# Gathering the small matmuls of a recurrence into longer runs in a two-layer decoder trunk

## The chip, the cores and the metric

The kernel runs on one core of a Trainium2 chip. The metric is the device time of one execution in microseconds (us). A core has a matrix engine (PE, with its weight loads shown as PEld), a vector engine (DVE), a scalar engine (ACT), a general engine (POOL) and DMA queues, of which most here are issued from SP. Each engine works through its own list of instructions in order and waits on semaphores for the others.

## The reference, cut to what matters

Two residual layers over 1024 tokens of width 1024, each with an RMSNorm that is shifted and scaled from a conditioning vector, followed by a final norm. Layer 0 has one input projection, from which eight heads of a delta-rule recurrence and a gated spatial mixer are fed; layer 1 is sliding-window attention. The change lies in the recurrence:

```
def step(S, inp):
    r_t, w_t, k_t, v_t, kk_t, a_t = inp
    sa = einsum('bhvk,bhk->bhv', S, -kk_t)
    S = S * w_t + sa * (kk_t * a_t) + v_t * k_t      # per head, 64 x 64
    y_t = einsum('bhvk,bhk->bhv', S, r_t)
    return S, y_t
```

The kernel computes it in blocks of 64 tokens: what happens inside a block becomes matrix products, and only the state goes from block to block.

## The kernel before, in words

**Units.** The recurrence is cut into 8 units: 4 pairs of heads (`j`) times 2 halves of the sequence (`half`), unit `un = 2*j + half`. A unit holds 8 blocks of 64 tokens and two heads, one head on partitions 0 to 63 and the other on 64 to 127 (`rows2`).

**Stages of a unit.** `front` (L493) prepares scaled inputs (tiles `AR`, `BK`, `SV`, `BR`, `PA`). `solve` (L595) makes the products `A`/`pM<-AR,BK`, then inverts a triangular matrix per block: DVE transposes into `LN` (L632), runs 15 steps of forward substitution (`pr`, `LT`, L645 and L646) and makes `ZT` (L650) and `Zq` (L653); PE then multiplies `pM<-ZT`, `pM<-Zq,M`, and after another DVE step, `Tq` (L681), `pM<-Tq`. In between it issues `p<-SV,AV` (L655 and on). `prep` (L709) makes the products `uw`, `mq` and `pn`. `scan` (L743) walks along the blocks: for each it multiplies the state with `AR[:, 0]` into the PSUM tile `chain`, and one DVE instruction (L758, a scalar_tensor_tensor into `PA`) makes the next state of it. This is called a hop. The output of a block, `py`, is the sum of two products, `AR[:, 1] x PA` (rows `py<-PA,AR`) and `BR x SV` (rows `py<-SV,BR`), one of each per head. `post` (L767) normalises `py`.

**Shapes.** The projections (`pproj` in layer 0, `op` in the output projections) are matmuls of 128x128 by 128x512 in fp32r; each leaves one row in the trace. The products of the recurrence are small plain fp32 matmuls: `chain`, `py<-PA,AR` and `p` have 64 rows and 64 columns, `py<-SV,BR` and `pn` 128 rows and 64 columns. Each fp32 matmul leaves two rows in the trace, so that "x4" in a row of the timeline is two matmuls.

**What sets the order.** In layer 0 the order of PE's list is made by a small planner in the kernel, `drive` (L1109). The stages are Python generators ("threads") with priorities: scan 0, prep and solve 1, fronts 2, the mixer's tails 4, the conditioning sums and output weights 5, the stream of input projections (`stream`, L912) 6, the output projection 7. A thread runs until it yields; `yield x` means that it is not called again before the planner's own clock has gone on by `x`; that clock goes forward by a cost per matmul (`cost`, L109). `yield 0.0` lets others in at once. When the small work has run up a debt over `LAT["debt"]`, the next ready projection goes ahead of it. So the projections fill what the stages leave: every projection matmul yields. Between two hops there is a `yield LAT["hop"]` of 1.3. The order of DVE's, ACT's and POOL's lists is made by the framework's scheduler from priorities, not by this planner.

**Lines that the change touches.** The yields at L661 (inside `p`), L668 (inside `pM<-ZT`), L718 (after each group of `uw`), L730 (after each group of `mq`), L739 (inside `pn`), and the loop of `scan`, L751 to L764.

Layer 1 and the output projections are not touched.

Of the kernel before, what the change touches and what calls it, by code (L numbers as in the profile page):

```python
# [11 lines left out]
F32 = mybir.dt.float32  # L12
# [3 lines left out]
ALU = mybir.AluOpType  # L16
# [4 lines left out]
P = 128  # L21
D = 1024
T = 1024
KC = 8
HT = 512
# [68 lines left out]
def tile_kernel(ctx, tc, x, cons, par, rows, ada, ada0, ew, wup, sgw, sgb, ewo, ow, owo, out, dbg=None):  # L94
# [14 lines left out]
    def cost(lhsT, rhs):  # L109
        n = math.prod(rhs.shape[1:])  # L110
        m = math.prod(lhsT.shape[1:])
        if rhs.dtype == F32R:
            return max(n if n >= 256 else 4 * n, m) / 2400.0
        return max(4 * n, 2 * m, 60) / 2400.0

    def mm(out, lhsT, rhs, **kw):
        clock[0] += cost(lhsT, rhs)
        last[0] = nc.tensor.matmul(out, lhsT=lhsT, rhs=rhs, **kw).ins  # L118
# [5 lines left out]
    V = nc.vector  # L124
# [8 lines left out]
    ps = pes.enter_context(tc.tile_pool(name="ps", bufs=2, space=PSUM, reuse_waits="tile"))  # L133
# [4 lines left out]
    def pm(name):  # L138
        return ps.tile([P, HT], F32, name=name, tag="m", bufs=2)
# [4 lines left out]
    def psc(name):  # L144
        return ps.tile([P, HT], F32, name=name, tag="sc", bufs=1)
# [128 lines left out]
            yield 0.0  # L274
        return pt

# [1 line left out]
    hp = ctx.enter_context(tc.tile_pool(name="hp", bufs=1, reuse_waits="tile"))  # L278

    def new_hh(half):  # L280
# [2 lines left out]
    def new_h():  # L283
        return [new_hh(half) for half in range(2)]

    h = new_h()
# [169 lines left out]
    y0d = dp.tile([P, KC, T], F32, name="y0d")  # L456
    gated = dp.tile([2, D], F32, name="gated")

# [1 line left out]
    gls = ExitStack()  # L460
    gl = gls.enter_context(tc.tile_pool(name="gl", bufs=1, reuse_waits="tile"))
    res = ExitStack()
# [5 lines left out]
    def RC(name, w):  # L468
        return rcon[:, CONSTS[name] - NC0:CONSTS[name] - NC0 + w]
# [3 lines left out]
    Sst = lp.tile([P, 64], F32, name="Sst")  # L473
    i2 = lp.tile([P, 64], F32, name="i2")
    G.tensor_tensor(out=i2, in0=ident[:, 0:64], in1=ident[:, 64:128], op=ALU.add)
    rows2 = (slice(0, 64), slice(64, 128))
# [118 lines left out]
    def solve(un):  # L595
        AR, BK = us[un]["AR"], us[un].pop("BK")
        yield LAT["sv0"]
        yield lambda: scannable[0] > un
        SV, BR, PA = (us[un][k] for k in ("SV", "BR", "PA"))
# [10 lines left out]
        for g in range(2):  # L610
            cg = slice(g * 4, g * 4 + 4)
            pts = [pm("A"), pM()]
            for i in range(4):
                c = g * 4 + i
                for hd in range(2):
                    hs = rows2[hd]
# [25 lines left out]
        for i in range(1, 16):  # L642
# [8 lines left out]
                        in1=RC("bm", 2).unsqueeze(2).unsqueeze(3).to_broadcast([P, 2, 8, 16]), op=ALU.mult)  # L651
# [5 lines left out]
        for c in range(8):  # L657
            for e in range(2):
                mm(pt[rows2[e], c * 64:c * 64 + 64], lhsT=AV[rows2[1 - e], c, :], rhs=SV[rows2[1 - e], c, e, :], start=True, stop=True, tile_position=(64 - e * 64, e * 64))
            if c == 3:  # L660
                yield 0.0  # L661
        S.activation(PA[:, :, 0, :], pt.rearrange("p (c v) -> p c v", c=8), AF.Copy)
        yield LAT["qt2"]
        p1 = pM()
        p2 = p1[:, 256:384].rearrange("p (c t) -> p c t", t=16)
        for c in range(8):
            if c == 4:
                yield 0.0  # L668
            for qd in range(4):
                a = qd * 32  # L670
                mm(p1[a:a + 32, c * 32:c * 32 + 32], lhsT=Df[a:a + 16, 112 + c * 16:144 + c * 16], rhs=ZT[a:a + 16, c, :], start=True, stop=True, tile_position=(a, a))
# [37 lines left out]
    def prep(un):  # L709
        u = us[un]  # L710
        AR, SV, BR, PA, dC = (u[k] for k in ("AR", "SV", "BR", "PA", "dC"))
        for g in range(2):
            cg = slice(g * 4, g * 4 + 4)
            pt = pm("uw")
            for i in range(4):
                mm(pt[:, i * P:(i + 1) * P], lhsT=Z[:, g * 4 + i, :], rhs=PA[:, g * 4 + i, :, :], start=True, stop=True)
            p4 = pt.rearrange("p (c a v) -> p c a v", c=4, a=2)
            yield 0.0  # L718
            S.activation(PA[:, cg, 1, :], p4[:, :, 1, :], AF.Copy)
            S.activation(SV[0:64, cg, 0, :], p4[0:64, :, 0, :], AF.Copy)  # L720
            S.activation(SV[64:128, cg, 1, :], p4[64:128, :, 0, :], AF.Copy)
        wdone[0] = un + 1
        yield LAT["uw"]
        for g in range(2):
            cg = slice(g * 4, g * 4 + 4)
            pt = pm("mq")
            for i in range(4):
                for e, hs in enumerate(rows2):
                    mm(pt[hs, i * P:(i + 1) * P], lhsT=PA[hs, g * 4 + i, 1, :], rhs=BR[hs, g * 4 + i, e, :, :], start=True, stop=True)
            yield 0.0  # L730
            p4 = pt.rearrange("p (c a v) -> p c a v", c=4, a=2)
            V.tensor_tensor(out=AR[:, 0, cg, :], in0=p4[:, :, 0, :], in1=i2.unsqueeze(1).to_broadcast([P, 4, 64]), op=ALU.add)
            V.tensor_tensor(out=AR[:, 1, cg, :], in0=p4[:, :, 1, :], in1=AR[:, 1, cg, :], op=ALU.add)
        pn = pm("pn")
        for c in range(8):
            for e, hs in enumerate(rows2):
                mm(pn[hs, c * 64:c * 64 + 64], lhsT=BR[:, c, e, 0, :], rhs=SV[:, c, e, :], start=True, stop=True)
            if c == 3:
                yield 0.0  # L739
        V.tensor_tensor(out=PA[:, :, 0, :], in0=pn.rearrange("p (c v) -> p c v", c=8), in1=dC.unsqueeze(2).to_broadcast([P, 8, 64]), op=ALU.mult)  # L740
        yield LAT["mq"]

    def scan(un):  # L743
        half, u = un % 2, us[un]
        AR, SV, BR, PA, dC = (u[k] for k in ("AR", "SV", "BR", "PA", "dC"))
        if half:
            V.tensor_copy(PA[:, 0, 1, :], Sst)
        else:
            V.tensor_copy(PA[:, 1, 1, :], PA[:, 0, 0, :])
        yield LAT["hop"]  # L750
        py = ps.tile([P, HT], F32, name="py", tag="y", bufs=1)  # L751
        pc = psc("chain")
        for c in range(8):
            yc = slice(c * 64, c * 64 + 64)
            if c >= 1 - half and c < 8 - half:
                for hs in rows2:
                    mm(pc[hs, yc], lhsT=AR[hs, 0, c, :], rhs=PA[hs, c, 1, :], start=True, stop=True)
                V.scalar_tensor_tensor(out=PA[:, c + 1, 1, :] if c < 7 else Sst, in0=pc[:, yc], scalar=dC[:, c:c + 1], in1=PA[:, c, 0, :], op0=ALU.mult, op1=ALU.add)  # L758
            for e, hs in enumerate(rows2):
                if c or half:  # L760
                    mm(py[hs, yc], lhsT=AR[hs, 1, c, :], rhs=PA[hs, c, 1, :], start=True, stop=False)
                mm(py[hs, yc], lhsT=BR[:, c, e, 1, :], rhs=SV[:, c, e, :], start=not (c or half), stop=True)
            if c < 7:
                yield LAT["hop"]  # L764
        return py

    def post(un, py):  # L767
# [198 lines left out]
    def solve_thread():  # L966
        for un in range(8):
            yield lambda: solvable[0] > un
            yield from prioritised(solve(un), BOOST)
            solved[0] = un + 1  # L970

    def scan_gen(un):
        py = yield from scan(un)
        scanned[0] = un + 1
        threads.append([1, post_gen(un, py), clock[0], None])
# [10 lines left out]
    def prep_thread():  # L986
        for un in range(8):
            yield lambda: solved[0] > un
            yield from prioritised(prep(un), BOOST)
            prepped[0] = un + 1  # L990
# [15 lines left out]
            yield from do_ada(layer, part)  # L1006
        done["ada"] = True

# [1 line left out]
    x1d = dp.tile([T, D], F32, name="x1d")  # L1010
    done = {}
    stored = [0]
# [133 lines left out]
    if "x1" in dbg:  # L1146
        nc.sync.dma_start(out=dbg["x1"], in_=x1d)

# [1 line left out]
    h = done["h1"]  # L1150
    ps = ctx.enter_context(tc.tile_pool(name="ps1", bufs=2, space=PSUM, reuse_waits="tile"))

# [4 lines left out]
    y = ypl.tile([P, KC, T], F32, name="y1")  # L1157
# [154 lines left out]
        for j in range(8):  # L1312
            nc.sync.dma_start(out=dbg["y1"][j], in_=y[:, j, :])

# [1 line left out]
    def half_tiles(name, tag, bufs, src, dt=F32):  # L1316
        ts = [at.tile([P, HT], dt, name=name, tag=tag, bufs=bufs) for n in range(2)]
        for n in range(2):
            nc.scalar.dma_start(out=ts[n], in_=src(slice(n * HT, (n + 1) * HT)))
        return ts  # L1320
# [95 lines left out]
```

## Time and profile before

| | |
|---|---|
| time of three runs | 1151.12, 1145.09 and 1151.21 us, median 1151.12 |
| profiled execution, first to last instruction | 1148.8 us; the page gives no time outside it |
| PE busy | 1083.1 us, 94% |
| DVE busy | 720.4 us, 63% |
| ACT busy | 526.8 us, 46% |
| POOL busy | 385.0 us, 34% |
| layer 0's stages | about 75 to 640 us of the span |
| the eight scans | the first chain matmul starts at 165.8 us, the last at 608.6 us |

The times are from one profiled execution. Busy is the time in which at least one instruction of the engine was under way; matmuls overlap, so that the cost of one is read from the distance between starts and not from its duration. In a row of the timeline stand the start, the duration, engine, line, operation, output and inputs, rows and columns, element count and number of rows merged, and in brackets the idle time ahead of it and what ended that. All matmuls of the helper `mm` stand under L118.

### The profile page before, as it was taken

To read this page: it belongs to the slowest core of one execution; us is meant where nothing else is said; L and a number is where in the kernel's file an instruction comes from. 1 tells how busy PE (TensorE), PEld (TensorE's weight loads), DVE (VectorE), ACT (ScalarE), POOL (GpSimd) and SP (SyncE) were. 2 spreads that over 40 slices of the span, in tenths; PEclk is the share of its full clock that TensorE was granted. 3 is DMA by queue.
4 is the path that set the end of the run, shared out by engine and by line. 5 is a ranking of instruction groups with operands and counts; after the bars stand their busy time and mean duration, and the time that the engine had idled before them with its cause. 6 is when DMAs were issued, how large, how long until landed. Compare 5 with 4: busy or idle time off the path is not lost.

```text
span 1148.8 us, 20773 instructions
## 1 busy us (share of the span) xinstructions
PE 1083.1 (94%) x7912; PEld 856.7 (75%) x7912; DVE 720.4 (63%) x1666; ACT 526.8 (46%) x1252; POOL 385.0 (34%) x474
## 2 busy tenths in 40 slices
PE   3799899999999998999999999999999999999997
PEld 2677677777776766677676778878888888878886
DVE  6966758575868584676735257774656654479754
ACT  5565435544454435354332122233656654477521
POOL 3652214131313222143234210024455554457301
PEclk7799999999999998999999999999999999999999
DMA  8710212112121211123333144331011001152131
GB/s 307 250 44 19 75 40 73 56 47 65 47 77 38 90 56 48 42 79 104 110 128 111 64 147 138 114 111 55 19 37 38 29 29 56 38 169 72 67 108 55
DMA packets 55131, 93.42 MB, mean 81 GB/s; under 512 B 5748, under 2 KB 15988, under 8 KB 55032
## 3 DMA queue, kind: packets, MB, share of 16 engines
q1 hardware_dynamic: 45032, 77.10, 20.6%
q10 hardware_dynamic: 10000, 15.01, 4.0%
q8 instruction: 62, 1.02, 0.4%
q14 instruction: 37, 0.30, 0.1%
HBM read 79.49 MB, written 12.59 MB: 80 GB/s over the span
## 4 chain that ended last, share of the span: by engine, by line
PE 80%; DVE 12%; ACT 4%; DMA 2%; issue 1%; POOL 1%; ACTq 0%; POOLq 0%; DVEq 0%; SPq 0%
PE pproj L118 38%; PE op L118 15%; PE py L118 5%; PE pM L118 2%; PE pS L118 2%; DVE acc L369 2%; PE po L118 2%; PE pT L1227 2%; PE uw L118 1%; PE mq L118 1%; PE chain L118 1%; PE p L118 1%; PE pn L118 1%; DVE adacc L848 1%; PE A L118 1%
## 5 line engine op out<-in xcount | busy, mean ns | idle before, releaser
L118 PE MATMUL pproj<-lo,whi 128*128 128x512 f32 x704 | 285.6, 406 | 0.0
L118 PE MATMUL pproj<-hi,whi 128*128 128x512 f32 x704 | 284.7, 404 | 0.7 <-ACT vt L1181 0.7
L118 PE MATMUL pproj<-hi,wlo 128*128 128x512 f32 x704 | 284.5, 404 | 0.3 <-POOL wlo L246 0.3
L246 POOL TENSOR_TENSOR wlo<-wraw,whi 128x512 fp32r<-128x512 f32 x86 | 115.7, 1366 | 209.3 <-ACT whi L245 206.2
L118 PEld LDWEIGHTS pproj<-hi,wlo 128*128 128x128 f32 x704 | 132.6, 188 | 28.5 <-issue 3.3
L118 PEld LDWEIGHTS pproj<-hi,whi 128*128 128x128 f32 x704 | 132.7, 189 | 27.0 <-ACT vt L1181 1.1
L118 PEld LDWEIGHTS pproj<-lo,whi 128*128 128x128 f32 x704 | 132.7, 188 | 26.4 <-issue 2.4
L245 ACT ACTIVATE whi<-wraw 128x512 fp32r<-128x512 f32 x102 | 58.9, 623 | 80.3 <-PE htp L122 31.6
L118 PE MATMUL op<-wo,whi 128*128 128x512 f32 x256 | 81.8, 400 | 1.7 <-ACT whi L245 1.7
L1217 ACT ACTIVATE Sx<-Sx,nm 128x257 f32<-128x257 f32 (+1 forms) x128 | 62.3, 489 | 27.2 <-DVE nm L1213 25.5
L1213 DVE CUSTOM_DVE_ANT_0 Sx<-pS,bias,nsink 128x256 f32<-128x256 f32 (+1 forms) x128 | 53.4, 463 | 30.7 <-PE pS L118 29.2
L1221 POOL TENSOR_SCALAR Sx<-Sx,rc 128x256 f32<-128x256 f32 (+1 forms) x128 | 60.0, 483 | 25.9 <-DVE rc L1219 21.4
L1233 DVE TENSOR_TENSOR PL<-pT,PH 128x512 fp32r<-128x512 f32 (+1 forms) x64 | 41.6, 654 | 30.2 <-ACT PH L1232 29.6
L848 DVE SCALAR_TENSOR_TENSOR adacc<-araw,cond,adacc 128x512 f32<-128x512 f32 x56 | 45.2, 808 | 22.5 <-DMA araw<-ada 22.4
L118 PEld LDWEIGHTS op<-wo,whi 128*128 128x128 f32 x256 | 48.8, 191 | 13.8 <-ACT whi L245 2.2
L118 PE MATMUL op<-hi,yh 128*128 128x512 f32 (+1 forms) x136 | 51.8, 381 | 0.4 <-ACT yh L1331 0.4
L118 PE MATMUL op<-hi,yl 128*128 128x512 f32 (+1 forms) x136 | 51.8, 381 | 0.4 <-DVE yl L1332 0.4
L118 PE MATMUL op<-wo,wlo 128*128 128x512 f32 x128 | 52.0, 406 | 0.0
L118 PE MATMUL op<-lo,yh 128*128 128x512 f32 (+1 forms) x136 | 51.6, 379 | 0.0
L213 POOL TENSOR_TENSOR st<-st,nhalf 128x1 f32<-128x1 f32 x16 | 10.4, 650 | 100.3 <-DVE st L212 100.3
L1232 ACT ACTIVATE PH<-pT 128x512 fp32r<-128x512 f32 (+1 forms) x64 | 35.7, 563 | 17.9 <-PE pT L1227 16.6
L1227 PE MATMUL pT<-con,Sx 128*128 128x128 f32 x240 | 41.2, 273 | 0.0
(310 smaller groups left out, 2257.9 us busy)
## 6 DMA issues: line engine op xcount, KB each, us to landing
araw<-ada SPq DMA_DIRECT2D x64, 256.0 KB, 2.8
wraw<-ew SPq DMA_DIRECT2D x50, 256.0 KB, 3.0
wraw<-ow SPq DMA_DIRECT2D x36, 256.0 KB, 2.9
adaraw<-ada SPq DMA_DIRECT2D x16, 512.0 KB, 5.9
x<-x SPq DMA_DIRECT2D x8, 512.0 KB, 5.6
woraw<-ewo SPq DMA_DIRECT2D x16, 256.0 KB, 3.2
xr<-x ACTq DMA_DIRECT2D x16, 256.0 KB, 3.5
wraw<-y0d SPq DMA_DIRECT2D x16, 256.0 KB, 3.3
```

The costliest lines, as they stand in the source:

```text
L118: last[0] = nc.tensor.matmul(out, lhsT=lhsT, rhs=rhs, **kw).ins
L213: G.tensor_tensor(out=st[:, 3:4], in0=st[:, 2:3], in1=nhalf[:, 0:1], op=ALU.pow)
L245: a = S.activation(hi[:, gs, :], raws[g], AF.Copy)
L246: b = E.tensor_tensor(out=lo[:, gs, :], in0=raws[g], in1=hi[:, gs, :].bitcast(F32), op=ALU.subtract)
L369: V.scalar_tensor_tensor(out=acc, in0=raw[:, i], scalar=c, in1=acc, op0=ALU.mult, op1=ALU.add)
L848: op = V.scalar_tensor_tensor(out=acc, in0=raw, scalar=cond[:, k:k + 1], in1=acc, op0=ALU.mult, op1=ALU.add)
L1213: V.tensor_tensor_reduce(out=Sx[:, e, off:2 * P], in0=pS3[:, e, 0:nk], in1=bias[e][:, off:], scale=1.0, scalar=nsink[:, hd:hd + 1], op0=AL ...
L1217: S.activation(pr[:, e, off:2 * P + 1], Sx[:, e, off:2 * P + 1], AF.Exp, bias=nm[:, e:e + 1], scale=-1.0, accum_out=sm[:, e:e + 1])
L1221: G.tensor_scalar(out=pr[:, e, off:2 * P], in0=pr[:, e, off:2 * P], scalar1=rc[:, e:e + 1], scalar2=0.5, op0=ALU.mult, op1=ALU.mult)
L1227: nc.tensor.transpose(pT4[:, kb, e, :], pr[:, e, kb * P:(kb + 1) * P], ident)
L1232: S.activation(PH[:, ks, :], pT2[:, ks, :], AF.Copy)
L1233: V.tensor_tensor(out=PL[:, ks, :], in0=pT2[:, ks, :], in1=PH[:, ks, :].bitcast(F32), op=ALU.subtract)
```

## The change

It takes five yields out, and writes the loop of `scan` in another order. A hop now holds the two chain matmuls and the DVE instruction alone. The 16 products `BR x SV` of a unit, which don't depend on the state, are issued in one batch in the hop of block 4, right behind its chain matmuls; the PSUM tile `py` is taken there. The 16 products `AR[:, 1] x PA` (14 in the first half of a sequence, where the first block has no state) come in one batch after the last hop and add onto the first batch. Only the first two matmuls of the first batch carry the start flag, and only the last two of the second batch the stop flag. The number of matmuls is the same, 6020 in PE's list.

```diff
         for c in range(8):
             for e in range(2):
                 mm(pt[rows2[e], c * 64:c * 64 + 64], lhsT=AV[rows2[1 - e], c, :], rhs=SV[rows2[1 - e], c, e, :], ...)
-            if c == 3:
-                yield 0.0
...
         for c in range(8):
-            if c == 4:
-                yield 0.0
             for qd in range(4):
...
-            yield 0.0
             S.activation(PA[:, cg, 1, :], p4[:, :, 1, :], AF.Copy)
...
-            yield 0.0
             p4 = pt.rearrange("p (c a v) -> p c a v", c=4, a=2)
...
                 mm(pn[hs, c * 64:c * 64 + 64], lhsT=BR[:, c, e, 0, :], rhs=SV[:, c, e, :], start=True, stop=True)
-            if c == 3:
-                yield 0.0
...
-        py = ps.tile([P, HT], F32, name="py", tag="y", bufs=1)
         pc = psc("chain")
-        for c in range(8):
+        for c in range(1 - half, 8 - half):
             yc = slice(c * 64, c * 64 + 64)
-            if c >= 1 - half and c < 8 - half:
-                for hs in rows2:
-                    mm(pc[hs, yc], lhsT=AR[hs, 0, c, :], rhs=PA[hs, c, 1, :], start=True, stop=True)
-                V.scalar_tensor_tensor(out=PA[:, c + 1, 1, :] if c < 7 else Sst, ...)
-            for e, hs in enumerate(rows2):
-                if c or half:
-                    mm(py[hs, yc], lhsT=AR[hs, 1, c, :], rhs=PA[hs, c, 1, :], start=True, stop=False)
-                mm(py[hs, yc], lhsT=BR[:, c, e, 1, :], rhs=SV[:, c, e, :], start=not (c or half), stop=True)
+            for hs in rows2:
+                mm(pc[hs, yc], lhsT=AR[hs, 0, c, :], rhs=PA[hs, c, 1, :], start=True, stop=True)
+            V.scalar_tensor_tensor(out=PA[:, c + 1, 1, :] if c < 7 else Sst, ...)
+            if c == 4:
+                py = ps.tile([P, HT], F32, name="py", tag="y", bufs=1)
+                for i in range(8):
+                    for e, hs in enumerate(rows2):
+                        mm(py[hs, i * 64:i * 64 + 64], lhsT=BR[:, i, e, 1, :], rhs=SV[:, i, e, :], start=i == 0, stop=False)
             if c < 7:
                 yield LAT["hop"]
+        for c in range(1 - half, 8):
+            for hs in rows2:
+                mm(py[hs, c * 64:c * 64 + 64], lhsT=AR[hs, 1, c, :], rhs=PA[hs, c, 1, :], start=False, stop=c == 7)
         return py
```

Two places show what it does to the lists. First PE's list in the scan of the last unit, before: one whole hop with the projections on either side.

```order
L118 MATMUL pproj<-hi,whi 128x512
L118 MATMUL chain<-PA,AR 64x64 x2
L118 MATMUL py<-PA,AR 64x64
L118 MATMUL py<-SV,BR 64x64
L118 MATMUL py<-PA,AR 64x64
L118 MATMUL py<-SV,BR 64x64
L118 MATMUL pproj<-lo,whi 128x512
```

The same scan in the changed kernel, the hops of blocks 4 and 5 (`adag` is a sum of the conditioning).

```order
L118 MATMUL chain<-PA,AR 64x64 x2
L118 MATMUL py<-SV,BR 64x64 x16
L118 MATMUL pproj<-hi,whi 128x512
L118 MATMUL pproj<-lo,whi 128x512
L118 MATMUL pproj<-hi,wlo 128x512
L118 MATMUL adag<-adacc,ones 1x512
L118 MATMUL chain<-PA,AR 64x64 x2
```

The four single `py` matmuls of a hop are gone from it, and one run of 16 stands in the hop of block 4.

Second DVE's list in the solve of the fifth unit, between the making of `Zq` and that of `Tq`, before (`mx` and `uT` belong to the mixer, `sqy` to `post`).

```order
L653 STREAM_TRANSPOSE Zq<-ZT 128x256
L835 SCALAR_TENSOR_TENSOR mx<-mix,prm,bst 128x512
L836 TENSOR_TENSOR uT<-mx,uT 128x512
L491 TENSOR_TENSOR sqy<-py,niy 128x512
L679 TENSOR_TENSOR Zq<-Zq,pM 128x8x16
L687 COPY Z<-Zq 32x8x32 x2
L681 STREAM_TRANSPOSE Tq<-Zq 128x256
```

The same stretch in the changed kernel, from `Zq` on (`krv` is an evacuated projection, `adacc` a conditioning sum, `bv` and `gz` belong to `post` and `front`).

```order
L653 STREAM_TRANSPOSE Zq<-ZT 128x256
L303 SCALAR_TENSOR_TENSOR krv<-pproj,prm,krv 128x511
L842 SCALAR_TENSOR_TENSOR adacc<-araw,cond,adacc 128x512
L829 SCALAR_TENSOR_TENSOR mx<-mix,prm,bst 128x512
L830 TENSOR_TENSOR uT<-mx,uT 128x512
L775 SCALAR_TENSOR_TENSOR bv<-yc,der,bv 128x512
L976 SCALAR_TENSOR_TENSOR gz<-bv,der,gz 128x512
L592 TENSOR_TENSOR bv<-bon,krv 128x512
```

Between `Zq` and the addition to it (`Zq<-Zq,pM`) three instructions stood before, and in the changed kernel ten do: the seven shown, then another `adacc` and the two instructions of another `krv`.

More of the change, by code (lines that the diff above doesn't have):

```diff
@@ L750, in scan @@
         yield LAT["hop"]
-        py = ps.tile([P, HT], F32, name="py", tag="y", bufs=1)
         pc = psc("chain")
-        for c in range(8):
+        for c in range(1 - half, 8 - half):
             yc = slice(c * 64, c * 64 + 64)
-            if c >= 1 - half and c < 8 - half:
-                for hs in rows2:
-                    mm(pc[hs, yc], lhsT=AR[hs, 0, c, :], rhs=PA[hs, c, 1, :], start=True, stop=True)
-                V.scalar_tensor_tensor(out=PA[:, c + 1, 1, :] if c < 7 else Sst, in0=pc[:, yc], scalar=dC[:, c:c + 1], in1=PA[:, c, 0, :], op0=ALU.mult, op1=ALU.add)
-            for e, hs in enumerate(rows2):
-                if c or half:
-                    mm(py[hs, yc], lhsT=AR[hs, 1, c, :], rhs=PA[hs, c, 1, :], start=True, stop=False)
-                mm(py[hs, yc], lhsT=BR[:, c, e, 1, :], rhs=SV[:, c, e, :], start=not (c or half), stop=True)
+            for hs in rows2:
+                mm(pc[hs, yc], lhsT=AR[hs, 0, c, :], rhs=PA[hs, c, 1, :], start=True, stop=True)
+            V.scalar_tensor_tensor(out=PA[:, c + 1, 1, :] if c < 7 else Sst, in0=pc[:, yc], scalar=dC[:, c:c + 1], in1=PA[:, c, 0, :], op0=ALU.mult, op1=ALU.add)
+            if c == 4:
[3 more added lines that the diff above has]
+                        mm(py[hs, i * 64:i * 64 + 64], lhsT=BR[:, i, e, 1, :], rhs=SV[:, i, e, :], start=i == 0, stop=False)
             if c < 7:
                 yield LAT["hop"]
+        for c in range(1 - half, 8):
+            for hs in rows2:
+                mm(py[hs, c * 64:c * 64 + 64], lhsT=AR[hs, 1, c, :], rhs=PA[hs, c, 1, :], start=False, stop=c == 7)
         return py
```

## Prediction

> **What bounds the kernel now.** I read the page first, for the span, the busy shares and the engines of the chain that ended last.
>
> ```profile
> span 1148.8 us, 20773 instructions
> PE 1083.1 (94%) x7912; PEld 856.7 (75%) x7912; DVE 720.4 (63%) x1666; ACT 526.8 (46%) x1252; POOL 385.0 (34%) x474
> PE 80%; DVE 12%; ACT 4%; DMA 2%; issue 1%; POOL 1%; ACTq 0%; POOLq 0%; DVEq 0%; SPq 0%
> ```
>
> PE is the bound: it works for 94% of the span and carries 80% of the chain. That is an average over stages, so I read the table by windows for layer 0, where the change lies. Its columns are the stretch, its length, then busy time of PE, PEld, DVE, ACT and POOL, and the granted PE clock.
>
> ```profile
> 200.00:320.00 120.00, 116.08 (x1185) 86.25 (x1184) 80.42 (x188) 55.64 (x129) 30.85 (x23) 1.00 0.17 54
> 440.00:560.00 120.00, 113.76 (x1048) 82.94 (x1047) 75.14 (x173) 50.43 (x117) 34.52 (x25) 0.96 0.23 73
> ```
>
> PE is busy for 114 to 116 of 120 us there, DVE for 75 to 80. So a microsecond of PE's work that goes in this stage comes off the end, unless PE then waits for DVE.
>
> Busy does not mean well used. The timeline of PE shows one hop of a scan with the projections around it.
>
> ```profile
> 545.52 0.39 PE L118 MATMUL pproj<-hi,wlo 128*128 128x512 f32 x1
> 545.75 0.39 PE L118 MATMUL pproj<-hi,whi 128*128 128x512 f32 x1
> 546.07 0.33 PE L118 MATMUL chain<-PA,AR 64*64 64x64 f32 x4
> 546.24 0.28 PE L118 MATMUL py<-PA,AR 64*64 64x64 f32 x2
> 546.44 0.33 PE L118 MATMUL py<-SV,BR 128*64 128x64 f32 x2
> 546.70 0.32 PE L118 MATMUL py<-PA,AR 64*64 64x64 f32 x2
> 546.96 0.33 PE L118 MATMUL py<-SV,BR 128*64 128x64 f32 x2
> 547.21 0.50 PE L118 MATMUL pproj<-lo,whi 128*128 128x512 f32 x1
> 547.55 0.40 PE L118 MATMUL pproj<-hi,wlo 128*128 128x512 f32 x1
> ```
>
> A projection starts 0.23 us after the one before. From 545.75 to 547.55 two such steps would take 0.46; it takes 1.80, so the hop costs 1.34. The four single `py` matmuls, 546.24 to 547.21, take 0.97 of it: 0.20 to 0.26 each, whenever the row count changes between 64 and 128. The same shapes in unbroken runs are far cheaper. Eight `pn` matmuls between projections, and 16 `p` matmuls:
>
> ```profile
> 583.39 0.51 PE L118 MATMUL pproj<-hi,whi 128*128 128x512 f32 x1
> 583.83 0.69 PE L118 MATMUL pn<-SV,BR 128*64 128x64 f32 x16
> 584.45 0.50 PE L118 MATMUL pproj<-lo,whi 128*128 128x512 f32 x1
> 584.78 0.39 PE L118 MATMUL pproj<-hi,wlo 128*128 128x512 f32 x1
> 541.37 1.15 PE L118 MATMUL p<-SV,AV 64*64 64x64 f32 x32
> 542.45 0.50 PE L118 MATMUL pproj<-lo,whi 128*128 128x512 f32 x1
> ```
>
> Eight take 0.62 to the next start and 16 take 1.08, so one more of its kind costs 0.46 / 8 = 0.058 us. The groups by form, for the whole kernel, give the number of matmuls (two rows each) and their busy time:
>
> ```profile
> L118 PE MATMUL py<-SV,BR 128*64 128x64 f32 x256 | 40.8, 246 | 0.0
> L118 PE MATMUL py<-PA,AR 64*64 64x64 f32 x240 | 36.3, 231 | 0.0
> L118 PE MATMUL pn<-SV,BR 128*64 128x64 f32 x256 | 11.0, 228 | 0.0
> ```
>
> `pn` multiplies as many matrices of the same shape as `py<-SV,BR` and is busy for 11.0 us against 40.8.
>
> **The change part by part.** The price of a hop that holds its two chain matmuls alone has no row. The nearest is two matmuls of one form between projections:
>
> ```profile
> 163.38 0.39 PE L118 MATMUL pproj<-hi,wlo 128*128 128x512 f32 x1
> 163.70 0.34 PE L118 MATMUL py<-SV,BR 128*64 128x64 f32 x4
> 163.97 0.50 PE L118 MATMUL pproj<-hi,whi 128*128 128x512 f32 x1
> 164.31 0.39 PE L118 MATMUL pproj<-lo,whi 128*128 128x512 f32 x1
> ```
>
> 0.93 less two steps of 0.23 is 0.47. Of it 0.35 belong to coming from and going back to projections (0.47 less 2 x 0.058).
>
> *Removed from the scans:* 56 hops fall from 1.34 to 0.47, 48.7 us. In the four second halves block 7 has only `py`: 1.34 less the chain's 0.17 (546.07 to 546.24), 4.7 us. In the four first halves block 0 is the visit just priced, 1.9. Together 55.3.
>
> *Added:* 248 matmuls in batches at 0.058, 14.4; eight changes of form from the chain to the first batch at 0.26, 2.1; four last batches stand alone between projections (in the first halves they follow the chain matmuls, of the same form), 4 x 0.35 = 1.4. Together 17.9. Bounds for one batched matmul: 0.058 as in `p` and `pn`, 0.26 as in `py` now. I take 0.058, since `pn` is the same instruction as `py<-SV,BR` but for the flags, and projections that add onto a tile follow each other at their steady 0.23. Net of the scans 37.4.
>
> *The five other runs.* In the order `pn` was split in all 8 units and is whole in all; `p` was split in 4, `pM<-ZT` in 3, `mq` in 2, `uw` in 1. Two visits of eight cost 0.93 each (583.39 to 584.78 less two steps), one of 16 costs 0.93 + 0.46. A merge saves 0.47, and 18 of them 8.5. Only `pn` and `p` show this; for the other three forms I take the same.
>
> *Runs that now stand together.* The whole order has 380 stretches of projections before and 335 after. 22 of the 45 are accounted for (18 merges, 4 block-0 visits). The other 23, such as `pn` now straight behind `mq`, save between 0.35 - 0.26 = 0.09 and 0.35: 2 to 8 us, I take 3, nearer the low end because the neighbours differ in form.
>
> Sum: 37.4 + 8.5 + 3 = 49 us less work on PE, which makes 1148.8 - 49 = 1100.
>
> *What is late next.* DVE. Its work is not less. I read the table by windows for the seven stretches from a unit's `LN` to its `pM<-ZT`, units 2 to 8; two of the seven and the sum:
>
> ```profile
> 343.60:376.90 33.30, 32.53 (x252) 23.68 (x249) 28.50 (x69) 13.68 (x27) 14.47 (x10) 1.00 0.15 51
> 536.60:562.40 25.80, 25.80 (x200) 18.91 (x199) 21.63 (x59) 5.92 (x11) 9.01 (x6) 1.00 0.35 110
> sum 214.00, PE 208.66 PEld 150.83 DVE 176.00 ACT 81.61 POOL 77.74; mean PE 29.81 PEld 21.55 DVE 25.14 ACT 11.66 POOL 11.11
> ```
>
> DVE is busy in 176 of 214 us. A scan lies in each stretch, so PE's 208.7 fall by about 37.4 / 8 + 0.24 = 4.9 each, 35 in all, to 174. Were DVE's list the same, PE would stand there. In the changed order DVE's lists between `LN` and `ZT` hold 370 instructions in these units instead of 411; at 28.50 / 69 = 0.41 each, 17 us move out, and DVE needs 159 of 174. The slack falls from 33 to 15 us, and not evenly: units 3, 5 and 7 keep 59, 61 and 58 instructions, and between `Zq` and `Tq` the fifth now has ten others where it had three. What slack of 33 let through, the groups of waits tell, and who waits in the hops:
>
> ```profile
> PE pM L118 <- DVE Tq L681: 8.1, 4, 2.8
> DVE PA L758 <- PE chain L118: 32.2, 31, 2.9
> ```
>
> New waits at `ZT` and `Tq`: at best 8 us go with the present ones, at worst all 35 are given back; I take 12, a third. Behind a `pM` that waits stands all of PE's list, the projections too.
>
> *The hops themselves.* The chain matmuls of one hop, DVE's answer, and an instruction of DVE of the wide kind:
>
> ```profile
> 165.78 0.33 PE L118 MATMUL chain<-PA,AR 64*64 64x64 f32 x4
> 166.16 0.28 DVE L758 SCALAR_TENSOR_TENSOR PA<-chain,dC,PA 128x64 f32<-128x64 f32 x1
> 563.10 0.72 DVE L848 SCALAR_TENSOR_TENSOR adacc<-araw,cond,adacc 128x512 f32<-128x512 f32 x1
> ```
>
> The distance between hops falls from 2.95 (1.34 and seven steps of 0.23) to 2.1. In 31 of 56 hops DVE was waiting for the chain, so there is no queue ahead of it. In the other 25 a DVE instruction of about 0.72 us may stand ahead; 0 to 18 us, I take 3, since the state is there 0.66 us after the hop's start (166.16 + 0.28 - 165.78) and 1.4 of the 2.1 are spare.
>
> *The clock.* One wait of the present four was followed by a lower granted clock:
>
> ```profile
> 443.17 0.63 PE L118 MATMUL pM<-Tq,N 32*32 32x32 f32 x6 [2.71 <-DVE Tq L681]
> 440.00:454.00 14.00, 11.20 (x102) 9.35 (x101) 4.47 (x7) 6.30 (x16) 2.42 (x2) 0.63 0.23 76
> 570.35 0.69 PE L118 MATMUL pM<-Tq,N 32*32 32x32 f32 x32 [2.75 <-DVE Tq L681]
> 560.00:640.00 80.00, 74.51 (x640) 56.45 (x639) 38.41 (x65) 25.85 (x53) 31.72 (x23) 1.00 0.41 129
> ```
>
> (1 - 0.63) x 14 = 5.2 us were lost after the first wait of 2.7 us, while the clock stayed at 1.00 from 560 to 640, around the wait of 2.75 us. With more waits I expect one more such loss or none: -5 to +10, I take 3. [...]
>
> Forecast: 1100 + 12 + 3 + 3 = 1118 us. The median of the three runs lies 2.3 above the profiled span, less than my terms are known to; I leave it out. A measurement of this kernel can tell about 0.5%, 6 us, from no change.
>
> **Rivals.** *DVE takes all of the stretches.* The 35 us come back as waits at `ZT` and `Tq`: 1148.8 - 14 = 1135. For it: slack of 15 us in seven stretches with one in-order queue. Against: 41 instructions have left them.
>
> *No new wait.* The two `Tq` waits and the clock loss go as well, since both were chance meetings: 1100 - 8 - 5 = 1087, or 1095 if half of that. Against: three units keep their DVE load.
>
> *Slower, by the clock.* Each unit has two places where PE can wait on DVE, 16 in all. If PE, run short, stopped there for 2.7 us with the loss of 5.2 us each time, a stop costs 7.9 us, and beyond six stops the 49 us are gone; at eight it is 1100 + 63 = 1163. For it: slack halves. Against: one of the two long waits cost no clock, and no projection is scarce. [...]
>
> *It does not do what it says.* Matmuls that add onto an open `py` tile run no faster in a batch, at 0.2: 248 x 0.2 = 50, so the scans gain 55.3 - 50 - 2.1 - 1.4 = 2, the other runs 11.5, and waits of the size above take 12: 1147. Against: nothing in `pn`'s rows.
>
> **How the numbers follow.** Forecast with its neighbourhood 0.71, DVE takes all 0.14, no new wait 0.06, slower by the clock 0.05, no effect 0.04. Faster by over 0.5%: 0.71 + 0.14 + 0.06 = 0.91; within: 0.04; slower: 0.05. The range goes from 1098, the sum with hardly a wait, to 1136, all stretches given back; outside lie the two last cases, most of the no-wait case and little more.
>
> **What would show it.** `py` busy falls from 77 us to under 25 in the groups by form, a hop's visit reads about 0.47, `pn` stands as one x32 row, and layer 1 lasts as long as now. PE's waits for `ZT` and `Tq` grow from 8 us to about 20, DVE's wait for the chain shrinks. I am wrong if `py` in a batch steps at over 0.1 us, if hops wait for DVE by more than 10 us, or if waits elsewhere, such as for ACT, take the gain.

## The result, and the profile after

The changed kernel takes 1120.39 us (median of 4 runs, 1118.01 to 1120.78) against 1151.16 us for the kernel before (median of 4, 1145.09 to 1151.59). The ratio is 0.9746, with a 95% interval of 0.9718 to 0.9773: 2.5% faster, 31 us. The forecast was 1118 us.

The page of the changed kernel, the lines that answer to the three shown first of before:

```profile
span 1119.0 us, 20771 instructions
PE 1038.8 (93%) x7912; PEld 833.5 (74%) x7912; DVE 716.3 (64%) x1666; ACT 526.6 (47%) x1252; POOL 382.5 (34%) x474
PE 44%; DVE 1%; DMA 1%; ACT 0%; issue 0%; POOLq 0%; DVEq 0%; SPq 0%; ACTq 0%
```

PE's busy time fell by 44.3 us and the span by only 29.8, so PE now stands idle for longer. (The profiled run took 1120.78 us, 1.8 more than its span.) The chain was followed through less than half of the span here, so its shares can't be set beside those of before.

The change lies in layer 0, so the account is made there, from 75 us to the first matmul of the output projection. The windows of before and then of the changed kernel, one stretch each (length, then busy time of PE, PEld, DVE, ACT and POOL, then the granted clock):

```profile
75.00:661.80 586.80, 560.09 (x5226) 419.11 (x5225) 367.65 (x810) 249.60 (x561) 172.13 (x125) 0.99 0.22 68
```

```profile
75.00:634.30 559.30, 517.15 (x5230) 396.16 (x5229) 363.98 (x810) 250.26 (x561) 169.23 (x125) 0.98 0.23 71
```

From such a row three numbers follow. *Waits* are length less PE busy: 26.7 before, 42.2 after. *Clock* is half of the time for which the trace grants half the clock, taken from the single records, since the column has two digits: 5.1 before, 10.9 after. *Work* is PE busy less the clock's share: 555.0 before, 506.3 after. So the work fell by 48.7 us, waits took 15.4 back and the clock 5.8. What follows layer 0 went from 487.0 to 484.7 us (1148.8 - 661.8 and 1119.0 - 634.3). All the later tables use these three.

The split has limits. It counts half clock also while PE waits: counted only while PE is busy, 0.1 to 3.2 us pass from clock to work, depending on the kernel, so that differences in work of under 3 us are not told apart. And each split describes the one run that was profiled: the four runs of the changed kernel had a mean granted clock of 0.976 to 0.991, and the profiled one is that with 0.976.

*The matmuls.* The groups by form, after:

```profile
L118 PE MATMUL pn<-SV,BR 128*64 128x64 f32 x256 | 9.2, 224 | 1.2 <-DVE AR L727 0.8
L118 PE MATMUL py<-SV,BR 128*64 128x64 f32 x256 | 9.2, 225 | 0.0
L118 PE MATMUL py<-PA,AR 64*64 64x64 f32 x240 | 8.7, 220 | 0.3 <-DVE PA L748 0.3
```

The two `py` groups are busy for 17.9 us instead of 77.1, and `py<-SV,BR` now costs what `pn` costs. The timeline of PE, a first batch of 16, one hop, and a last hop with its batch of 14:

```profile
166.69 1.15 PE L118 MATMUL py<-SV,BR 128*64 128x64 f32 x32
167.77 0.50 PE L118 MATMUL pproj<-lo,whi 128*128 128x512 f32 x1
...
280.87 0.39 PE L118 MATMUL pproj<-lo,whi 128*128 128x512 f32 x1
281.19 0.33 PE L118 MATMUL chain<-PA,AR 64*64 64x64 f32 x4
281.45 0.50 PE L118 MATMUL pproj<-hi,wlo 128*128 128x512 f32 x1
281.78 0.39 PE L118 MATMUL pproj<-hi,whi 128*128 128x512 f32 x1
...
283.26 0.33 PE L118 MATMUL chain<-PA,AR 64*64 64x64 f32 x4
283.42 0.98 PE L118 MATMUL py<-PA,AR 64*64 64x64 f32 x28
284.34 0.50 PE L118 MATMUL pproj<-hi,whi 128*128 128x512 f32 x1
```

A hop costs 281.78 - 280.87 less two steps of 0.23, 0.45 us, where it cost 1.34. The 16 matmuls of a first batch take 1.08 to the next start, as `p` did. The 14 of a last batch, which add onto what the first batch wrote, take 0.92.

*The waits.* What PE waited for in layer 0 (total, times, longest), first two groups of before that the prediction did not show, then the changed kernel:

```profile
PE bkt L122 <- DVE BK L541: 3.0, 1, 3.0
PE pM L118 <- ACT N L628: 2.1, 6, 0.8
```

```profile
PE pM L118 <- DVE nsk L488: 5.4, 2, 3.1
PE pM L118 <- ACT N L628: 4.2, 6, 2.6
PE bkt L122 <- DVE BK L541: 4.1, 3, 2.7
PE pM L118 <- DVE Tq L677: 2.6, 3, 1.1
...
PE pproj L118 <- POOL wlo L246: 2.4, 2, 2.1
...
PE chain L118 <- DVE PA L748: 1.1, 3, 0.5
```

No group grew by much. There are 29 stops of over 0.5 us where there were 20, on DVE, ACT and POOL alike. The stop of 3.1 us put down to `nsk` is a `Tq` stop: the timeline of DVE ahead of it, and the matmul that waited.

```profile
303.33 0.28 DVE L675 TENSOR_TENSOR Zq<-Zq,pM 128x128 f32<-128x128 f32 x1
303.53 0.68 DVE L487 TENSOR_REDUCE nsk<-sqk 128x8 f32<-128x512 f32 x1
304.12 0.74 DVE L976 SCALAR_TENSOR_TENSOR gz<-bv,der,gz 128x512 f32<-128x512 f32 x1
304.90 0.59 DVE L683 COPY Z<-Zq 32x256 f32<-32x256 f32 x2
305.50 0.45 DVE L677 STREAM_TRANSPOSE Tq<-Zq 128x256 f32<-128x256 f32 x1
305.87 0.13 DVE L488 TENSOR_SCALAR nsk<-nsk 128x8 f32<-128x8 f32 x1
306.09 0.74 PE L118 MATMUL pM<-Tq,N 32*32 32x32 f32 x20 [3.13 <-DVE nsk L488]
```

The matmul reads `Tq`; `nsk` is only the DVE instruction that ended last ahead of it. Two strangers, `nsk` and `gz`, stood ahead of `Tq` and cost 1.4 us. The other `nsk` stop, 2.26 us at 431.8, is at a `pM<-Tq` too. The `nsk` and `Tq` groups together make 8.0 us, against 8.1 at `Tq` before.

*The solve stretches.* The same seven stretches as in the prediction, from `LN` to `pM<-ZT`, two and the sum:

```profile
339.00:372.70 33.70, 25.93 (x226) 18.74 (x228) 30.69 (x68) 17.53 (x35) 16.86 (x12) 0.95 0.24 77
517.40:542.10 24.70, 24.70 (x213) 18.02 (x216) 19.20 (x55) 6.58 (x12) 9.18 (x7) 0.95 0.33 106
...
sum 189.00, PE 173.03 PEld 127.34 DVE 161.31 ACT 81.25 POOL 72.51; mean PE 24.72 PEld 18.19 DVE 23.04 ACT 11.61 POOL 10.36
```

PE's 173.0 and DVE's 161.3 are what the prediction worked out (174 and 159). The first of the two is a stretch in which DVE is now the busier engine: PE is busy for 25.9 of 33.7 us, where before it was 32.5 of 33.3, and DVE for 30.7. The other is still full of PE's work.

*The clock.* The two longest spells at half clock, as windows around them:

```profile
300.00:318.00 18.00, 14.75 (x167) 11.94 (x156) 8.15 (x17) 7.34 (x19) 2.37 (x3) 0.72 0.14 46
509.00:521.00 12.00, 9.37 (x65) 6.60 (x63) 8.26 (x19) 5.58 (x16) 3.77 (x3) 0.72 0.35 111
```

(1 - 0.72) x 18 = 5.0 us went behind the wait of 3.13 us, and 3.4 us behind one of 2.63.

### The profile page after: what moved, and what is told of

It reads as the page before. It is cut to its first block, busy times and chain, and to the rows that moved or that the text cites. A ratio compares the mean times of both kernels' runs of the same rounds, so it can differ in the third digit from the quotient of the medians.

```text
span 1119.0 us, 20771 instructions
## 1 busy us (share of the span) xinstructions
PE 1038.8 (93%) x7912; PEld 833.5 (74%) x7912; DVE 716.3 (64%) x1666; ACT 526.6 (47%) x1252; POOL 382.5 (34%) x474
## 5 line engine op out<-in xcount | busy, mean ns | idle before, releaser
L118 PEld LDWEIGHTS pproj<-hi,wlo 128*128 128x128 f32 x704 | 133.4, 189 | 28.3 <-POOL wlo L246 3.3
L1211 ACT ACTIVATE Sx<-Sx,nm 128x257 f32<-128x257 f32 (+1 forms) x128 | 62.3, 489 | 27.7 <-DVE nm L1207 25.8
L842 DVE SCALAR_TENSOR_TENSOR adacc<-araw,cond,adacc 128x512 f32<-128x512 f32 x56 | 48.7, 869 | 27.5 <-DMA araw<-ada 27.3
L645 DVE TENSOR_TENSOR pr<-Lf,LT 128x2 f32<-128x2 f32 (+14 forms) x120 | 45.2, 376 | 2.6
```

The costliest lines, as they stand in the source:

```text
L645: V.tensor_tensor(out=pr[:, 0:nc_, 0:i + 1], in0=Lf[:, i:i + 1, 0:i + 1].to_broadcast([P, nc_, i + 1]), in1=LTt[:, 0:nc_, 0:i + 1], op=ALU ...
L842: op = V.scalar_tensor_tensor(out=acc, in0=raw, scalar=cond[:, k:k + 1], in1=acc, op0=ALU.mult, op1=ALU.add)
L1211: S.activation(pr[:, e, off:2 * P + 1], Sx[:, e, off:2 * P + 1], AF.Exp, bias=nm[:, e:e + 1], scale=-1.0, accum_out=sm[:, e:e + 1])
```

## The experiments

The theory: PE's work falls by its price per visit and per change of form, and what is given back is waits, above all for DVE, with the clock behind them. Its rivals are named with each pair. The table has every run, with layer 0 taken apart as above (each from one profiled run; the medians are of 4 to 10). What follows layer 0 took between 481.9 and 488.8 us in these profiles, though no run edits it, so a few us between two profiles mean little.

| kernel | median us | ratio to before | layer 0 | waits | clock | work |
|---|---|---|---|---|---|---|
| before | 1151.16 | | 586.8 | 26.7 | 5.1 | 555.0 |
| changed | 1120.39 | 0.9746 [0.9718, 0.9773] | 559.3 | 42.2 | 10.9 | 506.3 |
| yields alone | 1148.24 | 0.9989 [0.9966, 1.0013] | 592.1 | 32.0 | 13.7 | 546.5 |
| scan alone | 1134.86 | 0.9868 [0.9830, 0.9905] | 571.7 | 45.6 | 13.7 | 512.4 |
| sorted in the hop | 1126.53 | 0.9796 [0.9764, 0.9829] | 567.4 | 31.1 | 10.2 | 526.0 |
| crossed in the hop | 1151.04 | 1.0015 [0.9992, 1.0037] | 588.8 | 27.7 | 5.1 | 556.0 |
| changed, light DVE | 1109.90 | 0.9640 [0.9622, 0.9658] | 547.8 | 36.3 | 4.4 | 507.1 |
| before, light DVE | 1149.33 | 0.9978 [0.9958, 0.9999] | 589.1 | 24.7 | 11.3 | 553.1 |
| batch behind `pn` | 1130.86 | 0.9831 [0.9813, 0.9849] | 571.1 | 53.4 | 14.5 | 503.2 |
| longer pauses | 1121.14 | 0.9737 [0.9713, 0.9760] | 551.1 | 33.4 | 13.9 | 503.8 |
| pause before `kt` | 1137.51 | 0.9890 [0.9857, 0.9922] | 583.5 | 50.2 | 33.4 | 499.9 |
| `kt` and `qt1` | 1118.04 | 0.9707 [0.9681, 0.9733] | 555.5 | 39.8 | 11.9 | 503.8 |
| changed, again | 1122.19 | 0.9756 [0.9721, 0.9790] | 557.7 | 41.0 | 11.9 | 504.8 |

### The two halves of the change

The first kernel is the changed one with the scan of before, so that only the five yields are gone; the second is the kernel before with the new scan alone.

```diff
 # yields alone: after, with the loop of scan as before
-        for c in range(1 - half, 8 - half):
+        for c in range(8):
...
 # scan alone: before, with the loop of scan as after; the five yields stay
-        for c in range(8):
+        for c in range(1 - half, 8 - half):
...
```

> Only the five yields are taken out; the scan stays as before. Theory (going between projections and small matmuls costs PE about 0.35 us a visit): 34 stretches of projections fewer in the order, 18 of them merges at 0.47 us and 16 at 0.09 to 0.35, so 10 to 14 us less work on PE, and 2 to 4 us of new waits: span about 1140, ratio 0.990 to 0.995. Rival (only the forms inside a hop cost, visits are free): within 2 us of before.

> Only the scan's loop is written anew; the five yields stay. Theory: 37 us less work on PE and about 11 us of new waits, span about 1123, ratio 0.975 to 0.980; py busy for 18 us instead of 77. Rival (the two parts need each other, since the projections between the split runs were the cover for DVE): this alone gives clearly less wait and nearly all of the gain, under 1120.

The yields alone make no difference that can be told, 0.9989 [0.9966, 1.0013]; the theory's time was missed. Their work did fall by 8.5 us, and `pn` by form reads as in the changed kernel (9.2 us). In the profiled run waits took 5.3 and the clock 8.5; that run, 1151.25 us, lies 3 above the median of its ten. The windows of this kernel, layer 0 and its three longest spells at half clock:

```profile
75.00:667.10 592.10, 560.14 (x5246) 425.77 (x5244) 365.39 (x814) 252.41 (x563) 172.29 (x127) 0.98 0.22 69
440.00:454.00 14.00, 10.87 (x93) 8.71 (x93) 6.35 (x14) 4.32 (x11) 1.64 (x1) 0.63 0.25 77
530.00:541.00 11.00, 8.22 (x45) 6.22 (x46) 7.43 (x19) 5.18 (x16) 5.06 (x4) 0.69 0.46 143
620.00:630.00 10.00, 9.42 (x39) 6.30 (x38) 5.15 (x5) 4.52 (x9) 6.11 (x6) 0.66 0.32 97
```

PE's busy time is that of before to 0.1 us (560.14 and 560.09), because half clock stretches the matmuls by what the merges took off them: work fell by 8.5 us, and the clock's share rose from 5.1 to 13.7. (In the changed kernel a projection steps at 0.23 us where the trace grants the full clock, and at 0.42 to 0.43 from 307.68 to 309.38, in a spell at half clock.) Only the clock's column tells the two apart.

The scan alone gives 42.5 us less work, 5 more than forecast, and 1134.86 us, about 10 above what the theory gave for it (a span of 1123, to which 1.8 come): in the profiled run, the shortest of its four, waits rose by 18.9 us and the clock's loss by 8.5. So the theory holds for the work of both halves, nearly (8.5 + 42.5 = 51.0 against 48.7 together), and fails for the time of both: they save 3 and 16 us where both together save 31. What is given back is no fixed share of the gain.

### Why a `py` matmul was dear: change of form, or the add

The first kernel keeps all of a hop's matmuls in the hop and only sorts them by form. The second keeps the four changes of form, but lets no matmul follow the one that it adds onto: each pair is crossed with the other head's.

```diff
 # sorted: before, with
             for e, hs in enumerate(rows2):
-                if c or half:
-                    mm(py[hs, yc], lhsT=AR[hs, 1, c, :], ...)
+            if c or half:
+                for hs in rows2:
+                    mm(py[hs, yc], lhsT=AR[hs, 1, c, :], ...)
+            for e, hs in enumerate(rows2):
                 mm(py[hs, yc], lhsT=BR[:, c, e, 1, :], ...)
...
 # crossed: before, in the order AR x PA of head 0, BR x SV of head 1,
 # AR x PA of head 1, BR x SV of head 0
```

> Kernel before with the four py matmuls of a hop sorted: the two of 64 rows, then the two of 128. No batch, the same number of visits; 120 changes of form fewer. Theory (a change of form costs 0.2 us): 24 us less work on PE, 5 to 8 us of new waits, span 1130 to 1133, ratio about 0.985. Rival (it is the visit between projections, or the length of a run, that costs): no change, 1148.

> Kernel before with the four py matmuls of a hop crossed: the form still changes at each, but no matmul adds onto the words that the one ahead of it wrote. Theory (the change of form costs): no change, 1146 to 1152. Rival (a matmul that adds onto what the last one wrote has to wait for it): as much as 24 us less, 1130.

Sorting saves 29.0 us of work, 5 more than its theory gave, and about 24 us of time (0.9796 [0.9764, 0.9829]); crossing saves nothing (1.0015 [0.9992, 1.0037]), and its `py` groups read 40.8 and 36.3 us as before. The timeline of the sorted kernel, one hop:

```profile
530.41 0.39 PE L118 MATMUL pproj<-lo,whi 128*128 128x512 f32 x1
530.73 0.33 PE L118 MATMUL chain<-PA,AR 64*64 64x64 f32 x4
530.89 0.28 PE L118 MATMUL py<-PA,AR 64*64 64x64 f32 x4
531.11 0.34 PE L118 MATMUL py<-SV,BR 128*64 128x64 f32 x4
531.37 0.50 PE L118 MATMUL pproj<-hi,wlo 128*128 128x512 f32 x1
531.71 0.40 PE L118 MATMUL pproj<-hi,whi 128*128 128x512 f32 x1
```

The hop is 531.71 - 530.41 less two steps of 0.23, 0.84 us instead of 1.34: two changes between 64 and 128 rows are gone from each of 60 visits, 29.0 / 120 = 0.24 us each. So the price is the change of the row count, not the add onto an open tile. What PE does in these 0.24 us no run shows.

This small edit is worth more than it looks. With 13.6 us less work saved than by the new scan alone it is 8 us faster (1126.53 and 1134.86), and it has most of the time that the whole change saves.

### Do the waits come from DVE's load

Both kernels leave out seven of the eight pieces of the conditioning sums that run through layer 0 (the loads stay), so DVE has 44 us less to do in the changed kernel's layer 0 and 39 less in that of before.

```diff
-                if k:
-                    op = V.scalar_tensor_tensor(out=acc, in0=raw, scalar=cond[:, k:k + 1], in1=acc, ...)
-                else:
-                    op = V.tensor_scalar(out=acc, in0=raw, scalar1=cond[:, 0:1], ...)
-                paced(op)
+                if k == KC - 1:
+                    paced(V.tensor_scalar(out=acc, in0=raw, scalar1=cond[:, 0:1], ...))
```

> Changed kernel, leaving out the conditioning sums of seven of eight pieces (their loads stay): 56 wide instructions of 0.74 us, about 41 us, leave DVE's list in layer 0. Theory (PE's new waits come from DVE's load): waits of PE in layer 0 fall from 40 to 26 or less, span 1105 to 1110. Rival (they come from the order of the lists and from ACT and POOL, not from load): 1116 to 1121.

> Kernel before, leaving out the same sums. Theory (before, DVE had slack): it gains less than the changed kernel does from the same cut, 3 to 7 us, span 1142 to 1146. Rival (load matters to both alike): the same gain as in the changed kernel.

The windows of the changed kernel with a light DVE, then of before with it:

```profile
75.00:622.80 547.80, 511.48 (x5231) 392.81 (x5231) 320.43 (x754) 251.26 (x562) 167.79 (x126) 0.99 0.23 72
```

```profile
75.00:664.10 589.10, 564.41 (x5231) 424.10 (x5230) 328.73 (x754) 252.21 (x562) 169.09 (x126) 0.98 0.21 67
```

The changed kernel gains 10.5 us from it (1120.39 to 1109.90), the kernel before about 2 (0.9978 [0.9958, 0.9999]), less than the 3 to 7 of its theory. PE's work is the same within 2 us in both, so the gain is not work: in the two profiled runs it is waits (42.2 to 36.3) and clock (10.9 to 4.4). The clock's part is not shown, since over all four runs the mean granted clock is 0.981 with the light DVE and 0.982 without. The pair speaks for DVE's load having become a cost with the change; it is no proof, since a list that is only shifted moved the time by 15 us in a run below. It also shows how little the load explains: with 44 us taken off DVE, 36 of the 42 us of waits are still there, 10 more than before, where the theory said 26 or less.

### Another place for the batch, and pauses against the waits

The first kernel issues the batch of 16 already in `prep`, behind `pn`, which is of the same form. The others lengthen the planner's pauses where the changed kernel's waits stood: in the front ahead of the transposes into `kt` (which wait for ACT), in the solve between the two groups of `pM<-AR,BK`, the second of which waits for ACT's `N` (`qt1`), and ahead of `pM<-Tq` (`qt4`).

```diff
 # batch behind pn: after, with
+        py = u["py"] = ps.tile([P, HT], F32, name="py", tag="y", bufs=1)
+        for i in range(8):
+            for e, hs in enumerate(rows2):
+                mm(py[hs, i * 64:i * 64 + 64], lhsT=BR[:, i, e, 1, :], ...)
...
 # pause before kt: after, with
+        yield 1.2
         pt = pm("kt")
...
 # kt and qt1: that, and
-"qt1": 1.5
+"qt1": 2.1
 # longer pauses: both, and
-"qt4": 1.77
+"qt4": 2.6
```

> Changed kernel with the batch of 16 products BR x SV issued straight behind pn, which has the same form, instead of in the hop of block 4. Theory (the form's change costs): 8 changes of about 0.2 us go and 3 visits come, about 1 us less work, span 1116 to 1120, not told apart from the changed kernel. Rival (the batch stands in the way of the first hop or of the tile of post): slower than the changed kernel by over 4 us.

> Changed kernel with longer planner pauses at three places where PE waits: a pause of 1.2 ahead of kt, qt1 from 1.5 to 2.1, qt4 from 1.77 to 2.6, so that projections are issued there. Theory (the waits are places where the planner's pause is too short for what DVE and ACT need, and projections are to be had): the waits at kt, pM<-AR,BK and pM<-Tq, 18 us, fall under 5, span 1105 to 1111. Rival (DVE as a whole has no room, waits move elsewhere): 1116 to 1121.

> Changed kernel with one pause of 1.2 planner units ahead of the kt transposes, nothing else. Theory (a wait at a place with a missing pause is filled by projections, and the rest of the list stays as it is): the waits at kt, 5.5 us, go, span 1112 to 1115 and faster than the changed kernel by 0.3 to 0.6%. Rival (any shift of the planner's list makes as many new waits elsewhere as it takes away, as in the run with three longer pauses): the same as the changed kernel, 1117 to 1122.

> Changed kernel with the pause ahead of kt and qt1 from 1.5 to 2.1. Theory: the waits at kt and pM<-AR,BK, 9.7 us, go, span 1108 to 1112. Rival: the same as the changed kernel, 1117 to 1122, with the waits at other places.

> The changed kernel once more beside these two on the same chip: 1118 to 1121 by both theories, as the mark for the comparison of a few us. Where the granted clock falls to half should again be right behind waits of PE of 1.7 us or more.

*Behind `pn`* the work reads 3.1 us less, but 0.6 if half clock is counted only while PE is busy, and the time rises by 10 (0.9831 [0.9813, 0.9849] beside 0.9746 [0.9718, 0.9773]). The theory gave the time of the changed kernel and missed; the rival had the time right, but only 3.5 us of the waits are at `chain`, where it looked for them. The largest that are new:

```profile
PE pM L118 <- DVE ZT L650: 5.2, 2, 2.9
PE adag L118 <- DVE vn L814: 5.2, 1, 5.2
...
PE adag L118 <- DVE adacc L842: 4.5, 1, 4.5
```

Two stops at a conditioning matmul make 9.7 us and two at `ZT` 5.2; none of these groups stands among those of the changed kernel. None of the matmuls that wait belongs to the batch. That the 16 matmuls, issued earlier, let the planner bring `adag` and `pM<-ZT` forward past DVE's readiness is argued from the planner's rules only.

*The pauses.* With all three, the waits of the profiled run fell by 8.8 us and its layer 0 by 8.2. But that run, 1116.67 us, is the shortest of four, and what followed layer 0 was 4.1 longer in it; the median is that of the changed kernel (0.9737 [0.9713, 0.9760]). The theory that the waits can be taken out place by place missed: those at `kt` and for `N` are gone, but a `pM<-Tq` still waits for 4.7 us (put down to `gst`), others appeared (`mix` 5.8, `chain` 4.2), and the clock lost 13.9. With the one pause ahead of `kt` the work reads least of all and the time is 15 us more than that of the changed kernel timed beside it (1137.51 and 1122.19). Its window and its largest wait:

```profile
75.00:658.50 583.50, 533.27 (x5240) 409.79 (x5238) 375.49 (x814) 249.01 (x558) 173.75 (x126) 0.94 0.22 69
```

```profile
PE chain L118 <- DVE PA L749: 13.5, 10, 3.9
```

Here the hops wait for DVE after all, and the clock of 0.94 costs 33.4 us, more than the waits and the clock together that the change had added (21.2). Both its theory and its rival missed, and why this one pause sets the two lists so badly against each other is open. With `kt` and `qt1` the median is 1118.04, where the theory gave a span of at most 1112; its interval and those of both runs of the changed kernel overlap, so no version is shown to beat the change. The repeat of the changed kernel gives 1122.19 and a ratio of 0.9756 [0.9721, 0.9790]: the result holds.

## Why the prediction was right, point by point

*Less work on PE, 49 us: right, 48.7.* The price of a hop (0.47; measured 0.45), of a batched matmul (0.058; 16 in 1.08 us) and of `py` in all (under 25; 17.9) were read from rows of before, and each held. The parts inside were less exact. The scans were put at 37.4 and gave 42.5 alone; the 18 merges at 8.5 and the runs that now stand together at 3, and the yields alone gave 8.5 for both. The parts overlap by 2.3 us, and the errors cancel: that the sum came within 1 us is in part luck. The scans' other 5 us are in part nine more visits gone: PE's list in that kernel has 13 stretches of projections fewer than before, where the working counted 4 (1 to 3 us at its 0.09 to 0.35 each). The rest is open.

*New waits at `ZT` and `Tq`, 12 us: the size was right, the place was wrong.* Here the working failed. PE's waits rose by 15.4 us, where 12 and the hops' 3 had been allowed. But `Tq` stands at 8.0 as before, not near 20, and `ZT` has no stop at all. (The 8.1 of before had another source in part: about 3.8 of it are copies that took longer beside POOL, shown in the last section, and 1.1 of the 8.0.) The slack of DVE in the seven stretches did shrink as worked out, yet the planner also moved what PE does there: the order of both lists is new. That waits come wherever one engine's new order meets the other's is argued; the runs with a light DVE speak for DVE's load in some of them (5.8 us of waits), and the rest is spread over stops on three engines. The prediction's third sign of being wrong, waits elsewhere that take the gain, thus came true in part. That 12 was close to the sum is luck as far as `ZT` and `Tq` are concerned.

*Hops wait for DVE, 3 us: right, mis-sized a little,* 1.1 us for `chain`; DVE's own wait for the chain shrank from 32.2 to 11.7. The pause ahead of `kt` shows that this was no sure thing: 13.5 us there, in the same scan code.

*The clock, 3 us from a range of -5 to +10: 5.8 in the profiled run,* which had the lowest clock of the four. The range was needed, and too narrow for one: against before the other kernels lose between -0.7 and +28.3 us.

*The rest.* Layer 1 is unchanged to 2.3 us, as said. The 1.8 us between span and time were left out; with them the forecast would have been 1120.

*The rivals.* DVE takes all stretches (1135): seen in one stretch, 339 to 372.7 us, but not in the sum, 189.0 us with PE at 173.0. No new wait: refuted by 15.4 us. No effect, because adding onto an open tile is slow: refuted by the last batch, 14 in 0.92 us, and by the crossed kernel. Slower by the clock (1163): not in this kernel, but in the one with the pause ahead of `kt` the clock lost 33.4 us in the profiled run, and half of the gain was gone. The stop price in the prediction (2.7 and 5.2 us) was of the right kind; how many stops there are is what the planner's order decides.

## What to carry to other kernels

Count the changes of form and the visits in a bound engine's list and price them from the rows on either side: such a sum was good to 1 us in 50 here, and to 5 in its largest part, while the waits and clock losses that a reshuffled list brings could only be sized (21 us here, 1 to 52 in the others, over before), not placed. Try the small edit first: sorting a hop by row count had about 24 of the 31 us. Judge a small rearrangement by work, waits and clock apart, and over several runs: the yields alone look like no change and are, in the profiled run, 8.5 us of gain under 13.8 us of new stops and half clock. When a planner makes the order, try several orders with the same work and keep the one that runs fastest, since taking out one wait at a time moved it elsewhere each time.

## What the runs showed of the hardware that was not expected

*Half clock behind short waits.* Every spell at half clock that began in layer 0, from 75 us on, of before and of the changed kernel began within a wait of PE of at least 2.0 us or at most 0.7 us after one, and lasted 3.4, 6.8 or 10.2 us: in before 10.2 behind a wait of 2.71, in the changed kernel 10.2 behind a wait of 3.13, 6.8 behind 2.63, 3.4 behind 2.09. Waits of 3.03 and 2.75 us in before and of 2.66, 2.26 and 2.15 in the changed kernel had none. So the same wait does not cost the same each time: in the changed kernel one of 2.63 us was followed by 6.8 us of half clock and one of 2.66 by none. The repeat lost 11.9 us to the clock in its layer 0; behind which waits is not shown. Of the four runs of the changed program, the one with the highest mean clock, 0.991, was the shortest (span 1116.2 against 1118.3 to 1119.0).

*A short copy that took longer.* The `Tq` waits of 2.71 and 2.75 us in before were not DVE's queue alone. The timeline of DVE and of POOL ahead of the first, then of both ahead of the second, in before:

```profile
440.25 2.32 DVE L687 COPY Z<-Zq 32x256 f32<-32x256 f32 x2
442.58 0.45 DVE L681 STREAM_TRANSPOSE Tq<-Zq 128x256 f32<-128x256 f32 x1
```

```profile
437.72 3.43 POOL L246 TENSOR_TENSOR wlo<-wraw,whi 128x512 fp32r<-128x512 f32 x2
441.11 1.31 POOL L547 TENSOR_TENSOR qh<-qb,qh 128x512 fp32r<-128x512 f32 x1
```

```profile
567.08 2.67 DVE L687 COPY Z<-Zq 32x256 f32<-32x256 f32 x2
567.05 2.54 POOL L246 TENSOR_TENSOR wlo<-wraw,whi 128x512 fp32r<-128x512 f32 x2 [4.96 <-ACT whi L245]
```

The two copies took 2.32 us and ended at 442.57, as POOL's work did at 442.42; the second pair took 2.67 us and ended 0.16 after POOL's work. In the changed kernel, at 304.90, they took 0.59. So it is throughout the two traces: of the 32 such copies, 26 took 0.28 to 0.29 us each, and the six that took longer, 0.73 to 1.39, each ended 0.15 to 0.16 us after an instruction of POOL had ended. Two of the 26 ran beside POOL's small `grs<-gst` (128x8) and took 0.28 and 0.29 us. That POOL's instruction holds such a copy up is argued from these ends alone: no run here took it away.
